# Block 0 goes last in phase one, and its last two pairs' operands reach the resident tiles by copies on the chip

## The chip, the cores and the metric

The kernel runs on one core of a Trainium2 chip. Its time is the device time of one execution in microseconds (us); a kernel's figure is the median over its runs. Engines are named as in the profile: PE (TensorE matmuls), PEld (its weight loads), DVE (VectorE), ACT (ScalarE), POOL (GpSimd) and SP (SyncE, which here only starts transfers). A "q" behind a name, as SPq, is the engine's instruction queue.

## The reference, cut to what is computed

```python
def mixer_layer(x, pool_past, pos0, norm_g, w_in, ...):
    h = rmsnorm(x, norm_g)                                  # (T, 1024)
    u, v, z_a, xb, z_b = jnp.split(h @ w_in, ...)           # w_in is (1024, 5 * 1024)
    v_n = layernorm(v, ln_v_g, ln_v_b)
    a = u * chunk_mlp(v_n, w_spatial, b_spatial) * silu(z_a)  # 8 heads, 128x128 mixing of positions
    x_ext = concatenate([pool_past, xb])
    b = pool_mix(x_ext, pos0, w_pool, pool_scale) * silu(z_b) # trailing means over 2/4/8/16 rows
    return x + concatenate([a, b]) @ w_out, x_ext[-15:], v_n
...
y = rmsnorm(mixer_layer(x, ...)[0], final_g)
```

There is one layer, with 4096 prompt tokens and 32 sample tokens, all in float32.

## The kernel before, in words

Every large product is a two-by-two block product with seven multiplications instead of eight (`NQ = 7`, numbered q). Each float32 operand is split into a rounded part and a remainder (`lo_part`), and three matmuls per 128 rows of depth form one product. One multiplication q is therefore 4 x 3 = 12 matmuls, of 128 x 512 in most places; `Combine.after(q)` takes the sums out of PSUM with copies on ACT and additions on DVE.

**Phase one.** The weights of v lie in seven resident tiles, the `slots` (`wv[q]`, one for each q). The 4096 tokens are four blocks of 1024, and a block is four `Pair`s (b, j), j = 0 to 3, of 2 x 128 tokens. `Pair.operands()` transposes a pair's normed tokens on PE and makes seven operand tiles of 4 KB a partition from them (`split`, pool `op_p`, nine buffers). Each is stored to DRAM, to `xops` for blocks 0 to 2 and to `xops_l` for block 3, and is used for v (`Pair.product`). Rows of v are normed (`norms`) and stored to `v_all` from ACT's queue (`Pair.store`, tiles `vt` of pool `v_p`, four buffers). Pairs follow each other in the order of blocks 0, 1, 2, 3. The last two, `pa` and `pb`, are taken in the order of `lagged`: (a,0) (a,1) (b,0) (a,2) (b,1) (a,3) (b,2) (a,4) (a,5) (b,3) (a,6) (b,4) (b,5) (b,6). Then come their norms and stores.

**Phase two.** For each block, 1024 columns of tokens lie as operands in the same seven slots, loaded from `xops` (`Tokens.load`, two transfers of 1 MB for each slot). Sets of weights ("pool" and "gate") pass by them. A set's weights are loaded as `raw` tiles, and `prepare` turns them into operand tiles `wop`, up to `LEAD` = 5 multiplications ahead. Results go to `t` tiles (pool `t_p`). The first group is a pair of pool sets, `groups[0]`, in lagged order; behind its (b,3) stand the spatial constants (`WT`, `bias`). All pools of phase two are opened on memory that phase one has left, and a new tile waits for the old tiles that it covers.

**Phase three.** Out products: `OutPair`s of 2 x 128 rows times `w_out`, in two halves z of the depth. `OutPair.finish` norms both row tiles and stores them to the output. For the last pair `finish(True)` runs behind the last multiplication.

Engines run their queues in order; the order within a queue is fixed when the program is built, by a planner that may move an instruction ahead of others that are not ready by its own costs.

Of the kernel before, what the change touches and what calls it, by code (L numbers as in the profile page):

```python
# [35 lines left out]
def stream_step(ctx: ExitStack, tc, x_prompt, x_sample, state_pool, norm_g, w_in, ln_v_g, ln_v_b,  # L36
# [141 lines left out]
    def stacked(acc, rows, n, terms):  # L178
# [6 lines left out]
        mm(acc[:, :n], st, wh, start=False, stop=True)  # L185


    with ExitStack() as ph:
        xt_p = ph.enter_context(tc.tile_pool(name="xt_p", bufs=4))
        g_p = ph.enter_context(tc.tile_pool(name="g_p", bufs=1))  # L190
        h_p = ph.enter_context(tc.tile_pool(name="h_p", bufs=6))
        op_p = ph.enter_context(tc.tile_pool(name="op_p", bufs=9))
        v_p = ph.enter_context(tc.tile_pool(name="v_p", bufs=4))
        ps_acc = ph.enter_context(tc.tile_pool(name="ps_acc", bufs=5, space=bass.MemoryType.PSUM))
# [19 lines left out]

        g_bc = g_p.tile([P, D], F32, name="g_bc")


# [34 lines left out]
        def load_v_weights(c):  # L252
            v_raws[c] = a, b = [op(F32).rearrange("p (k e) -> p k e", e=P) for _ in range(2)]
            c0 = D + c * P
            nc.sync.dma_start(a, w_in_v[:, :, c0:c0 + P])
            nc.sync.dma_start(b, w_in_v[:, :, c0 + 512:c0 + 512 + P])
# [169 lines left out]
        class Pair:  # L426
            def __init__(self, b, j):
                self.b, self.j = b, j

# [15 lines left out]
            def split(self, q, src):  # L445
                t = op().rearrange("p (h x) -> p h x", h=2)
                self.ops[q] = t
                nc.scalar.copy(t[:, 0, :], src)
                lo_part(t[:, 1, :], src, t[:, 0, :])
                if self.b < NB - 1:  # L450
                    dst = xops[self.b, self.j].rearrange("p (q x) -> p q x", q=NQ)[:, q, :]
                    nc.sync.dma_start(dst, t.rearrange("p h x -> p (h x)").bitcast(F32))
                else:
                    dst = xops_l[q, :, :, self.j * P:(self.j + 1) * P]
                    nc.sync.dma_start(dst, t.rearrange("p h (k t) -> p (h k) t", t=P).bitcast(F32))
# [45 lines left out]

            def store(self):
                for z, v in enumerate(self.v):
                    dst = v_all[self.b, :, :, 4 * z + self.j, :].rearrange("h p c -> p h c")
                    nc.scalar.dma_start(dst, v.rearrange("p (h c) -> p h c", c=P))

        pairs += [Pair(b, j) for b in range(NB) for j in range(4)]
        before = {0: [past.load, edge_load, lambda: load_rows(2)], 1: [lambda: load_v_weights(0), lambda: load_rows(3)],
# [18 lines left out]
        for n, pair in enumerate(pairs[:-2]):  # L527
            steps = pairs[n + 1].operands()
            pair.start()
            for q in range(NQ):  # L530
# [7 lines left out]
                pair.product(q)  # L538
        pa, pb = pairs[-2:]
        steps = pb.operands()  # L540
        pa.start()
        pb.start()
        for n, (pair, q) in enumerate(lagged(pa, pb)):
# [5 lines left out]
            pair.product(q)  # L549
        for pair in (pa, pb):  # L550
            norms([], [(v, P) for v in pair.v])
            pair.store()


    def pool(name, bufs, stack=ctx, **kw):
        return stack.enter_context(tc.tile_pool(name=name, bufs=bufs, reuse_waits="tile", **kw))

    raw_p = pool("raw_p", 6)
    op_p = pool("wop_p", 6)
    sum_p = pool("sum_p", 3)  # L560
    ps_acc2 = pool("ps_acc2", 6, space=bass.MemoryType.PSUM)

# [36 lines left out]
    class OutPair:  # L599
# [50 lines left out]
        def multiply(self, q):  # L650
            own = {0: 0, 1: 1, 2: 0, 3: 3, 4: 0, 5: 5, 6: 3}[q]
            if own == q:
                self.acc[own] = acc2_tile()
            x, w = self.ops[q], w_slots[self.z, q]
# [14 lines left out]

        def finish(self, last=False):  # L670
            t0 = 2 * self.i * P
            if self.z == 0:
                for n in range(2):
                    nc.gpsimd.dma_start(part[t0 + n * P:t0 + (n + 1) * P, :], self.y[n])  # L674
                return
            a = small("ssa", 2)
            nc.vector.tensor_tensor(a, self.ss[:, :, 0], self.ss[:, :, 1], ALU.add)
            nc.vector.tensor_scalar(a, a, 1.0 / D, EPS, ALU.mult, ALU.add)
            r = rsqrt(a, 2)
            for n in range(2):  # L680
                y = self.y[n]
                for c in (slice(0, 512), slice(512, D)) if last else (slice(0, D),):
                    nc.vector.scalar_tensor_tensor(y[:, c], y[:, c], r[:, n:n + 1], f_bc[:, c], ALU.mult, ALU.mult)
                    (nc.sync if last and n == 0 else nc.gpsimd).dma_start(yp[t0 + n * P:t0 + (n + 1) * P, c], y[:, c])  # L684

# [50 lines left out]

    def acc2_tile():
        return ps_acc2.tile([P, 512], F32, tag="acc", name="acc")

    with ExitStack() as ph:  # L740
        t_p = pool("t_p", 10, ph)
        cn_p = pool("cn_p", 1, ph)
        ps_sp = pool("ps_sp", 1, ph, space=bass.MemoryType.PSUM)
        ps_acc = ps_acc2

        def acc_tile():
            return ps_acc.tile([P, 512], F32, tag="acc", name="acc")
# [7 lines left out]
        WT = cn_p.tile([P, HEADS, 2 * P], F32R, name="WT")  # L755
        bias = cn_p.tile([P, HEADS, P], F32, name="bias")
        bias_s = cn_p.tile([P, HEADS, DEC], F32, name="bias_s")

# [16 lines left out]
        def spatial_constants(ws, bsp):  # L775
# [6 lines left out]
            for z0 in (0, P):  # L782
                nc.gpsimd.memset(WT[64:P, :, z0:z0 + 64].bitcast(F32), 0.0)
            for q in range(2):
# [47 lines left out]
        class Set:  # L832
# [4 lines left out]

            def load(self):
                i = self.i
# [9 lines left out]
                for view in views:  # L849
                    raws.append(raw_tile().rearrange("p (k e) -> p k e", e=P))  # L850
                    nc.sync.dma_start(raws[-1], view)
                self.load_v()
# [181 lines left out]

        prepare(1)
        for q in range(NQ):
            tokens[0].load(q)
        prepare(LEAD)
        constants_loaded = spatial_loads()
        at, later = 0, []  # L1040
# [31 lines left out]
    with ExitStack() as ph:  # L1072
# [47 lines left out]
        for n in range(n_sets, len(groups)):  # L1120
# [6 lines left out]
            for m, (s, q) in enumerate(order):  # L1127
                at += 1
                prepare(at + LEAD)
                if m == 0 and n in samples:  # L1130
                    samples[n].load()
                k = n - n_sets - 4
                if 0 <= k < KT and m in (0, 2):
                    state_load(k) if m == 0 else state_split()
                s.multiply(q)
                if m == 2 and ended:
                    for x in ended:
                        x.finish()
# [7 lines left out]
            if g[0].z == 0 and len(g) == 2:  # L1146
                kept, ended = [x.y for x in g], None
        for x in ended:
            x.finish(True)

# [28 lines left out]
```

## Time and profile before

| | us |
|---|---|
| median of 3 runs (lowest, highest) | 2444.87 (2441.67, 2445.24) |
| the profiled execution, own time | 2445.14 |
| its span, first to last instruction | 2443.4 |
| granted TensorE clock, mean | 0.991 |
| PE busy | 2382.9 (98% of the span), 11981 matmuls |
| DVE busy | 1865.1 (76%) |
| ACT busy | 964.7 (39%) |

The profile covers one execution. The granted clock is the share of full speed (2.4 GHz) that TensorE had; 0.50 is its lower level, 1.2 GHz. In the profile's rows "x44" counts instructions, an arrow in brackets names what ended an engine's idle time, and Lnnn is a line of the kernel before. Phase one ends at 424.5 us of the span, phase two at about 1776 us.

### The profile page before, as it was taken

The numbers are of one execution on the slowest core, as the hardware profiler recorded it, in microseconds if no ns is written. First come the engines' busy times: TensorE is split into PE (matmuls) and PEld (weight loads), VectorE is DVE, ScalarE is ACT, GpSimd is POOL, SyncE is SP. The second block draws the span as 40 slices with busy tenths as digits, with TensorE's granted clock in tenths as the row PEclk, the third lists the DMA queues.
The fourth block names the chain that finished last, engine by engine and source line by source line (L and its number), as shares of the span: only waits on it lengthen the run. The fifth ranks groups of instructions, "written<-read, shape, count | busy, mean of one in ns | idle before, by whom it ended". The sixth has DMA issues, their size and how long they took to land. (4 is left out here: it accounts for less than half of the span.)

```text
span 2443.4 us, 32978 instructions
## 1 busy us (share of the span) xinstructions
PE 2382.9 (98%) x11981; PEld 1995.0 (82%) x11981; DVE 1865.1 (76%) x3386; ACT 964.7 (39%) x1702; POOL 309.2 (13%) x462
## 2 busy tenths in 40 slices
PE   6999999899999999999999999999999999999997
PEld 5788887688878888788888799999987777888876
DVE  6887776687786877877778868678776777588886
ACT  5554453344433444433444334444322333233332
POOL 3200000011111111111112112222210000000000
PEclk8999999999999999999999999999999999999999
DMA  8677799733348323556234382335596776855542
GB/s 253 240 271 272 277 271 278 269 108 100 121 130 311 102 92 98 172 187 209 96 104 148 107 321 90 96 98 181 192 330 231 259 250 228 310 169 167 152 135 74
DMA packets 337082, 458.15 MB, mean 188 GB/s; under 512 B 19516, under 2 KB 256828, under 8 KB 334232
## 3 DMA queue, kind: packets, MB, share of 16 engines
q1 hardware_dynamic: 282296, 369.34, 45.0%
q0 software_dynamic: 20144, 65.62, 7.6%
q10 hardware_dynamic: 34480, 21.11, 3.0%
q8 instruction: 94, 1.54, 0.3%
q14 instruction: 68, 0.56, 0.1%
HBM read 280.04 MB, written 175.96 MB: 187 GB/s over the span
## 5 line engine op out<-in xcount | busy, mean ns | idle before, releaser
L174 PE MATMUL acc<-slot,wop 128*128 128x512 f32 (+1 forms) x2240 | 788.1, 352 | 11.3 <-ACT t L150 6.0
L176 PE MATMUL acc<-slot,wop 128*128 128x512 f32 (+1 forms) x2240 | 786.2, 351 | 1.4 <-DVE wop L82 1.4
L175 PE MATMUL acc<-slot,wop 128*128 128x512 f32 (+1 forms) x2240 | 785.6, 351 | 0.3 <-DMA slot<-xops 0.3
L174 PEld LDWEIGHTS acc<-slot,wop 128*128 128x128 f32 x2240 | 422.6, 189 | 74.1 <-ACT t L150 7.5
L82 DVE TENSOR_TENSOR wop<-raw,wop 128x512 fp32r<-128x512 f32 x510 | 359.1, 706 | 151.8 <-ACT wop L107 108.7
L176 PEld LDWEIGHTS acc<-slot,wop 128*128 128x128 f32 x2240 | 422.3, 189 | 61.8 <-DVE wop L82 1.9
L175 PEld LDWEIGHTS acc<-slot,wop 128*128 128x128 f32 x2240 | 422.7, 189 | 57.5 <-DMA slot<-xops 0.6
L657 PE MATMUL acc<-slot,wop 128*128 128x512 f32 x896 | 354.0, 395 | 3.8 <-DVE y L663 2.8
L658 PE MATMUL acc<-slot,wop 128*128 128x512 f32 x896 | 353.7, 395 | 0.0
L659 PE MATMUL acc<-slot,wop 128*128 128x512 f32 x896 | 353.6, 395 | 0.0
L107 ACT CAST wop<-raw 128x512 fp32r<-128x512 f32 x340 | 209.8, 621 | 281.5 <-PE acc L176 221.6
L663 DVE TENSOR_TENSOR y<-acc,y 128x512 f32<-128x512 f32 x256 | 173.7, 687 | 96.2 <-PE acc L659 95.1
L148 DVE TENSOR_TENSOR t<-acc,t 128x512 f32<-128x512 f32 (+1 forms) x320 | 184.3, 582 | 77.3 <-ACT t L157 56.3
L657 PEld LDWEIGHTS acc<-slot,wop 128*128 128x128 f32 x896 | 168.4, 188 | 46.6 <-issue 4.0
L659 PEld LDWEIGHTS acc<-slot,wop 128*128 128x128 f32 x896 | 168.4, 188 | 40.3
L658 PEld LDWEIGHTS acc<-slot,wop 128*128 128x128 f32 x896 | 168.4, 188 | 39.8
L619 ACT CAST wop<-raw 128x512 fp32r<-128x512 f32 x160 | 99.2, 621 | 240.6 <-PE acc L659 202.1
L174 PE MATMUL acc<-slot,op 128*128 128x512 f32 x448 | 181.5, 406 | 0.0
L176 PE MATMUL acc<-slot,op 128*128 128x512 f32 x448 | 177.2, 396 | 0.0
L175 PE MATMUL acc<-slot,op 128*128 128x512 f32 x448 | 176.7, 394 | 0.0
L107 ACT CAST wop<-sum 128x512 fp32r<-128x512 f32 x144 | 89.2, 620 | 212.5 <-PE acc L176 174.9
L82 DVE TENSOR_TENSOR wop<-sum,wop 128x512 fp32r<-128x512 f32 x208 | 142.7, 686 | 38.4 <-ACT wop L107 30.1
(218 smaller groups left out, 2885.5 us busy)
## 6 DMA issues: line engine op xcount, KB each, us to landing
raw<-in_w_in_dram SPq DMA_DIRECT2D x104, 512.0 KB, 4.4
xops<-op SPq DMA_DIRECT2D x84, 512.0 KB, 6.2
slot<-xops SPq DMA_DIRECT2D x42, 1024.0 KB, 11.2
abT<-t POOLq DMA_DIRECT2D x128, 256.0 KB, 2.6
raw<-abT SPq DMA_DIRECT2D x64, 512.0 KB, 4.3
wops<-wop SPq DMA_DIRECT2D x56, 512.0 KB, 3.9
slot<-wops SPq DMA_DIRECT2D x14, 2048.0 KB, 9.2
xt<-in_x_prompt_dram SPq DMA_DIRECT2D x32, 512.0 KB, 4.6
```

The lines of the kernel that those rows point to most:

```text
L82: nc.vector.tensor_tensor(out, src, hi.bitcast(F32), ALU.subtract)
L107: nc.scalar.copy(hi, src)
L148: add = lambda o, x, y: nc.vector.tensor_tensor(o, x, y, ALU.add)
L174: mm(acc, sh, mh, start=fresh and k == 0, stop=False, skip_group_check=True)
L175: mm(acc, sh, ml, start=False, stop=False, skip_group_check=True)
L176: mm(acc, sl, mh, start=False, stop=k == 3, skip_group_check=True)
L619: nc.scalar.copy(t[:, 0], src)
L657: mm(a, x[:, 0, k, :], w[:, k, 0], start=fresh and k == 0, stop=False, skip_group_check=True)
L658: mm(a, x[:, 0, k, :], w[:, k, 1], start=False, stop=False, skip_group_check=True)
L659: mm(a, x[:, 1, k, :], w[:, k, 0], start=False, stop=k == 3, skip_group_check=True)
L663: nc.vector.tensor_tensor(y, self.acc[bank], y, ALU.add)
```

## The change

Six edits. The pairs of phase one go through blocks 1, 2, 3, 0. The pairs (0,2) and (0,3), now the last two, no longer store their operands. Instead, as each slot comes free of `wv[q]`, `load_first(q)` loads the operands of (0,0) and (0,1) into it with two transfers of 512 KB and copies those of `pa` on DVE and those of `pb` on ACT; phase two starts with these slots. The four raw weight tiles of `groups[0]` are loaded from POOL's queue, and their preparation precedes the last norms and stores of v, which POOL issues too. The v tiles lie at the other end of memory and are given back only then, and `t_p`, `WT` and the biases are opened after that; one raw tile of the v weights takes a `vt` buffer instead of an `op` buffer. In phase three the last pair is ended in two parts: its first row tile behind the multiplication q = 5, its second behind q = 6, with halves of 512 columns stored from SP's and ACT's queues.

```diff
@@ pools of phase one
+    v_stack = ctx.enter_context(ExitStack())
+    v_p = pool("v_p", 4, v_stack, side="right")
...
-        v_p = ph.enter_context(tc.tile_pool(name="v_p", bufs=4))
...
-            v_raws[c] = a, b = [op(F32).rearrange("p (k e) -> p k e", e=P) for _ in range(2)]
+            v_raws[c] = a, b = [t.rearrange("p (k e) -> p k e", e=P)
+                                for t in (op(F32), op(F32) if c < 3 else vtile())]
@@ class Pair
-                self.b, self.j = b, j
+                self.b, self.j, self.direct = b, j, b == 0 and j >= 2
...
                 lo_part(t[:, 1, :], src, t[:, 0, :])
+                if self.direct:
+                    return
...
-            def store(self):
+            def store(self, queue=nc.scalar):
...
-                    nc.scalar.dma_start(dst, v.rearrange("p (h c) -> p h c", c=P))
+                    queue.dma_start(dst, v.rearrange("p (h c) -> p h c", c=P))
...
-        pairs += [Pair(b, j) for b in range(NB) for j in range(4)]
+        pairs += [Pair(b, j) for b in (1, 2, 3, 0) for j in range(4)]
@@ the last two pairs
+        def load_first(q):
+            first_ops[q] = t = slot()
+            dst = t[:, :8 * HALF].rearrange("p (h j x) -> p h j x", h=2, j=4)
+            src = xops[0].rearrange("j p (q h x) -> q h p j x", q=NQ, h=2)
+            for h in range(2):
+                nc.sync.dma_start(dst[:, h, :2].bitcast(F32), src[q, h, :, :2])
+            nc.vector.tensor_copy(dst[:, :, pa.j], pa.ops[q])
+            nc.scalar.copy(dst[:, :, pb.j], pb.ops[q])
...
             pair.product(q)
-        for pair in (pa, pb):
-            norms([], [(v, P) for v in pair.v])
-            pair.store()
+            if pair is pb:
+                load_first(q)
@@ OutPair.finish
-        def finish(self, last=False):
+        def finish(self, last=None):
...
+            tiles = (0, 1) if last is None else (last,)
...
-            for n in range(2):
+            for n in tiles:
                 y = self.y[n]
-                for c in (slice(0, 512), slice(512, D)) if last else (slice(0, D),):
-                    nc.vector.scalar_tensor_tensor(y[:, c], y[:, c], r[:, n:n + 1], f_bc[:, c], ALU.mult, ALU.mult)
-                    (nc.sync if last and n == 0 else nc.gpsimd).dma_start(yp[t0 + n * P:t0 + (n + 1) * P, c], y[:, c])
+                for z, c in enumerate((slice(0, 512), slice(512, D)) if last is not None else (slice(0, D),)):
...
+                    queue = nc.gpsimd if last is None else (nc.sync, nc.scalar)[z]
+                    queue.dma_start(yp[t0 + n * P:t0 + (n + 1) * P, c], y[:, c])
@@ phase two
-                nc.gpsimd.memset(WT[64:P, :, z0:z0 + 64].bitcast(F32), 0.0)
+                tc.keep_in_program_order(nc.gpsimd.memset(WT[64:P, :, z0:z0 + 64].bitcast(F32), 0.0))
...
-        prepare(1)
-        for q in range(NQ):
-            tokens[0].load(q)
+        tokens[0].ops = first_ops
+        for s in groups[0]:
+            loads.pop(0)[2].load(nc.gpsimd)
         prepare(LEAD)
+        for pair in (pa, pb):
+            norms([], [(v, P) for v in pair.v])
+            pair.store(nc.gpsimd)
+        v_stack.close()
+        t_p = pool("t_p", 10, ph)
...
@@ phase three
                 s.multiply(q)
+                if n == len(groups) - 1 and q == 5:
+                    s.finish(0)
...
-        for x in ended:
-            x.finish(True)
+        ended[0].finish(1)
```

## Rows read from the trace of the kernel before

**Rows 1.** Busy time of each engine over the whole span: time, share, instructions.

```profile
PE 2382.9 (98%) x11981; PEld 1995.0 (82%) x11981; DVE 1865.1 (76%) x3386; ACT 964.7 (39%) x1702; POOL 309.2 (13%) x462
```

**Rows 2.** Stretches: length, busy us (instructions) by engine, clock, DMA share, GB/s.

```profile
404.00:414.00 10.00, 10.00 (x44) 8.07 (x43) 3.68 (x6) 1.54 (x3) 0.00 (x0) 1.00 1.18 292
...
424.50:437.00 12.50, 10.32 (x36) 7.38 (x35) 12.02 (x32) 4.46 (x8) 0.00 (x0) 0.86 1.07 391
437.00:460.00 23.00, 17.02 (x66) 13.11 (x65) 4.75 (x7) 7.58 (x12) 1.53 (x7) 0.93 1.07 391
460.00:477.00 17.00, 15.63 (x69) 11.76 (x68) 16.10 (x43) 4.64 (x7) 1.57 (x7) 1.00 0.59 172
...
500.00:520.00 20.00, 19.81 (x96) 16.16 (x96) 17.97 (x27) 11.03 (x19) 3.70 (x4) 1.00 0.34 106
```

**Rows 3.** PE in order of time: start, length, instruction, idle time before it.

```profile
428.87 0.79 PE L176 MATMUL acc<-slot,wop 128*128 128x512 f32 x1 [1.44 <-DVE wop L82]
...
452.30 0.78 PE L174 MATMUL acc<-slot,wop 128*128 128x512 f32 x1 [4.78 <-ACT t L150]
```

**Rows 4.** Waits between 384 and 520 us: total, times, longest.

```profile
ACT t L150 <- DMA v_all<-vt: 7.2, 1, 7.2
```

**Rows 5.** Landing time of the v_all stores, all 32.

```profile
DMA to landing us min/median/max: 3.3/5.7/17.4
```

**Rows 6.** SP's queue in order of time.

```profile
394.17 0.38 SPq L825 DMA_DIRECT2D slot<-xops  x1
394.64 10.99 SPq L455 DMA_DIRECT2D xops_l<-op  x5
...
413.05 32.57 SPq L825 DMA_DIRECT2D slot<-xops  x13
```

**Rows 7.** Landing time of the slot loads from xops, all 42.

```profile
DMA to landing us min/median/max: 5.6/11.2/17.5
```

**Rows 8.** Transfers by line: queue, count, size of one, median us to landing.

```profile
raw<-in_w_in_dram SPq DMA_DIRECT2D x104, 512.0 KB, 4.4
...
xops_l<-xt POOLq DMA_DIRECT2D x7, 64.0 KB, 6.6
...
comb<-vt ACTq DMA_DIRECT2D x8, 512.0 KB, 2.9
...
out_dram<-y SPq DMA_DIRECT2D x2, 256.0 KB, 2.1
out_dram<-y POOLq DMA_DIRECT2D x2, 256.0 KB, 2.4
```

**Rows 9.** DVE by line and shape.

```profile
L405 DVE TENSOR_SCALAR h<-op 128x512 fp32r<-128x512 f32 x1 | 0.4, 427 | 1.1 <-PE acc L244 1.1
```

**Rows 10.** ACT by line.

```profile
L866 ACT CAST raw<-raw 128x1024 fp32r<-128x1024 f32 x32 | 33.7, 1053 | 6.0 <-DVE wop L82 5.4
```

**Rows 11.** DVE by line, 384 to 500 us.

```profile
L82 DVE TENSOR_TENSOR op<-tr,op 128x512 fp32r<-128x512 f32 x3 | 2.1, 686 | 0.9 <-ACT op L448 0.9
```

**Rows 12.** DVE in order of time, last group.

```profile
2413.34 0.16 DVE L90 TENSOR_TENSOR rs_t<-rs_y 128x2 f32<-128x2 f32 x1
2413.45 0.69 DVE L663 TENSOR_TENSOR y<-acc,y 128x512 f32<-128x512 f32 x1
...
2429.93 0.69 DVE L663 TENSOR_TENSOR y<-acc,y 128x512 f32<-128x512 f32 x1 [2.10 <-PE acc L659]
...
2434.04 2.74 DVE L683 SCALAR_TENSOR_TENSOR y<-y,rs_y,spare 128x512 f32<-128x512 f32 x4
```

**Rows 13.** POOL in order of time, last stores.

```profile
2436.41 1.21 POOL L684 DMA_DIRECT2D out_dram<-y  x2 [16.88 <-DVE y L683]
```

**Rows 14.** ACT in order of time, while the last v weights are made.

```profile
60.17 0.62 ACT L107 CAST slot<-op 128x512 fp32r<-128x512 f32 x1 [1.66 <-DMA op<-in_w_in_dram]
```

**Rows 15.** POOL in order of time, at the start.

```profile
32.68 1.26 POOL L103 TENSOR_TENSOR op<-op 128x512 f32<-128x512 f32 x1
```

**Rows 16.** DVE in order of time, at the start.

```profile
32.77 1.19 DVE L87 TENSOR_SCALAR rs_t<-na 128x2 int32<-128x2 int32 x1
```

More of the change, by code (lines that the diff above doesn't have):

```diff
@@ L185, in stacked, with pool @@
         mm(acc[:, :n], st, wh, start=False, stop=True)
+    def pool(name, bufs, stack=ctx, **kw):
+        return stack.enter_context(tc.tile_pool(name=name, bufs=bufs, reuse_waits="tile", **kw))
+    v_stack = ctx.enter_context(ExitStack())
+    v_p = pool("v_p", 4, v_stack, side="right")
     with ExitStack() as ph:
@@ L215, in stream_step @@
         g_bc = g_p.tile([P, D], F32, name="g_bc")
+        first_ops = {}
         rows_t, wraw = {}, []
@@ L549, in stream_step @@
             pair.product(q)
-        for pair in (pa, pb):
-            norms([], [(v, P) for v in pair.v])
-            pair.store()
-    def pool(name, bufs, stack=ctx, **kw):
-        return stack.enter_context(tc.tile_pool(name=name, bufs=bufs, reuse_waits="tile", **kw))
+            if pair is pb:
+                load_first(q)
     raw_p = pool("raw_p", 6)
@@ L560, in stream_step @@
     sum_p = pool("sum_p", 3)
-    ps_acc2 = pool("ps_acc2", 6, space=bass.MemoryType.PSUM)
+    ps_acc = pool("ps_acc2", 6, space=bass.MemoryType.PSUM)
     def raw_tile(dt=F32):
@@ L652, in multiply @@
             if own == q:
-                self.acc[own] = acc2_tile()
+                self.acc[own] = acc_tile()
             x, w = self.ops[q], w_slots[self.z, q]
@@ L675, in finish @@
                 return
+            tiles = (0, 1) if last is None else (last,)
             a = small("ssa", 2)
-            nc.vector.tensor_tensor(a, self.ss[:, :, 0], self.ss[:, :, 1], ALU.add)
+            ss, a = self.ss[:, tiles[0]:tiles[-1] + 1], a[:, :len(tiles)]
+            nc.vector.tensor_tensor(a, ss[:, :, 0], ss[:, :, 1], ALU.add)
             nc.vector.tensor_scalar(a, a, 1.0 / D, EPS, ALU.mult, ALU.add)
-            r = rsqrt(a, 2)
-            for n in range(2):
+            r = rsqrt(a, len(tiles))
+            for n in tiles:
                 y = self.y[n]
-                for c in (slice(0, 512), slice(512, D)) if last else (slice(0, D),):
-                    nc.vector.scalar_tensor_tensor(y[:, c], y[:, c], r[:, n:n + 1], f_bc[:, c], ALU.mult, ALU.mult)
-                    (nc.sync if last and n == 0 else nc.gpsimd).dma_start(yp[t0 + n * P:t0 + (n + 1) * P, c], y[:, c])
+                for z, c in enumerate((slice(0, 512), slice(512, D)) if last is not None else (slice(0, D),)):
+                    nc.vector.scalar_tensor_tensor(y[:, c], y[:, c], r[:, n - tiles[0]:n - tiles[0] + 1], f_bc[:, c],
+                                                   ALU.mult, ALU.mult)
+                    queue = nc.gpsimd if last is None else (nc.sync, nc.scalar)[z]
+                    queue.dma_start(yp[t0 + n * P:t0 + (n + 1) * P, c], y[:, c])
     class OutSample:
@@ L735, in multiply @@
             nc.gpsimd.dma_start(ys, self.y)
-    def acc2_tile():
-        return ps_acc2.tile([P, 512], F32, tag="acc", name="acc")
     with ExitStack() as ph:
[L741 to L747, printed above, removed]
         def temp(dt=F32):
@@ L753, in few @@
             return t_p.tile([P, HALO + DEC], F32, tag="few", name="few", bufs=3)
-        WT = cn_p.tile([P, HEADS, 2 * P], F32R, name="WT")
-        bias = cn_p.tile([P, HEADS, P], F32, name="bias")
-        bias_s = cn_p.tile([P, HEADS, DEC], F32, name="bias_s")
         def spatial_loads():
@@ L836, in __init__, with load @@
                 self.tok, self.kind, self.i, self.ops, self.stage = tok, kind, i, {}, tok.b
-            def load(self):
+            def load(self, queue=nc.sync):
                 i = self.i
@@ L850, in load @@
                     raws.append(raw_tile().rearrange("p (k e) -> p k e", e=P))
-                    nc.sync.dma_start(raws[-1], view)
+                    queue.dma_start(raws[-1], view)
                 self.load_v()
@@ L1033, in prepare @@
                 done += 1
-        prepare(1)
-        for q in range(NQ):
-            tokens[0].load(q)
+        tokens[0].ops = first_ops
+        for s in groups[0]:
+            loads.pop(0)[2].load(nc.gpsimd)
         prepare(LEAD)
+        for pair in (pa, pb):
[3 more added lines that the diff above has]
+        t_p = pool("t_p", 10, ph)
+        cn_p = pool("cn_p", 1, ph)
+        ps_sp = pool("ps_sp", 1, ph, space=bass.MemoryType.PSUM)
+        WT = cn_p.tile([P, HEADS, 2 * P], F32R, name="WT")
+        bias = cn_p.tile([P, HEADS, P], F32, name="bias")
+        bias_s = cn_p.tile([P, HEADS, DEC], F32, name="bias_s")
         constants_loaded = spatial_loads()
```

## The prediction

> **What bounds the kernel now.** The page's first part comes first: PE is busy 98% of the span [rows 1], so an edit can win only where PE stands still or runs at its lower clock. The table of stretches around the end of phase one, at 424.5 us, shows such a place. In an undisturbed stretch PE starts 44 matmuls in 10 us, one per 0.227 us. From 424.5 to 437 us it starts 36, worth 8.2 us, in 12.5: 4.3 lost. From 437 to 460 it starts 66, worth 15.0, in 23: 8.0 lost. From 460 to 477 it starts 69, worth 15.7, in 17: 1.3 lost [rows 2]. Idle time is one part of this; the granted clock's mean of 0.86 and 0.93 is the other: after each of the two long gaps PE ran at 1.2 GHz for a while. In the first stretch that cost (1 - 0.86) x 12.5 = 1.7 us [rows 2].
>
> PE in order of time gives the two gaps: 1.44 us until DVE has a remainder of a weight operand, 4.78 us until ACT's copy into a t tile has emptied a bank [rows 3]. The waits say what ACT stood for: 7.2 us for a store of v to DRAM [rows 4], since the t tile lies on an old v tile. The longest of these stores took 17.4 us where the median is 5.7 [rows 5]: from 424.5 to 460 us the DMA share is 1.07, at 391 GB/s [rows 2], that is, the DMA engines are full. SP's queue says with what, and why the weights were late: stores of the last pair's operands, each waiting for its operand, hold the queue from 394.64 until 405.6; only then come the four raw weight loads, and from 413.05 to 445.6 thirteen slot loads of 1 MB [rows 6].
>
> At the other end the last addition starts at 2429.93; its chain of small operations reaches the output multiplications at 2434.04, and POOL issues the last two stores from 2436.41 on [rows 12, 13].
>
> **The end of phase one, first stretch.** The two direct pairs drop 14 stores of 512 KB, and the slots take 7 MB from DRAM instead of 14. The stores that held SP are gone; the raw loads stand in POOL's queue, which is empty there. Their tiles lie on x tiles whose last transposes are over by about 391.4 us (one multiplication of 12 x 0.227 = 2.7 us ahead of 394.17, when the first slot comes free [rows 6]). They land 4.4 us after issue if they cost what they do on SP, 6.6 if they cost what POOL's transfers in 1024 pieces took [rows 8]; by 405 either way, some 20 us ahead of use. What can stay of the 4.3 us: the weight operands lie partly on op tiles that now live until their copy, the last copies end near 426, and five operands must be made while the copies run. I leave 0.8 us of the 4.3 (bounds 0 and 4.3): win 3.5.
>
> **Second stretch.** The new t tiles lie on op tiles, free once copied, not on v tiles, and with 14 MB of traffic less the stores of v no longer queue behind 13 MB of slot loads. The 8.0 us go, but DVE must follow: from 424.5 to 477 it was busy 12.02 + 4.75 + 16.10 = 32.9 us; if PE does the same in 52.5 - 12.3 = 40.2 us, DVE is at 82%. From 500 to 520 it was at 90%, and PE lost only 0.2 [rows 2]. So I leave 1.0 (bounds 0 and 8.0): win 7.0. The 1.3 us from 460 to 477 belong to the spatial constants, with DVE busy 16.1 of 17 [rows 2]; I leave them whole (bounds 0 and 1.3).
>
> **The added copies.** Seven copies of 1024 elements on DVE: the one SBUF-to-SBUF operation with one tensor input took 0.43 us for 512 [rows 9], so between that and 0.85; I take 0.7, 4.9 us in all. Seven on ACT at 1.05 [rows 10], 7.4 us. Over the 30 us of the last pair there is room: from 404 to 414 DVE was busy 3.68 of 10 and ACT 1.54 [rows 2]. If that room were not there, all 12.3 us could land on PE.
>
> One copy is on a tight path. Seven operands of pa and two of pb fill the nine op buffers, so operand 1 of pb must wait until `load_first(0)` has copied operand 0, and that waits for the slot, free at 394.17 [rows 6]. (b,1) is due one multiplication later, 2.7 us. ACT's copy 1.05, a cast of 512 (half of it, 0.53) and the remainder 0.69 [rows 10, 11] make 2.3, before hand-overs and whatever stands ahead in two queues. I take 0.3 us lost (bounds 0 and 1.5, one more cast and remainder ahead). Behind (b,1) PE alone waits; the later operands have two products or more.
>
> POOL also issues the four stores of v and then clears WT, which must wait for these stores. Behind that stand POOL's halo copies of the first pool sets; the first of these sets ends eleven multiplications, 30 us, after 424.5, so I cost this at nothing; were the stores as late as 17.4 us [rows 5] it would still be covered.
>
> A rule of the skill speaks against this arrangement. The start of the kernel shows the effect in one form: with POOL at a two-input operation of 1.26 us [rows 15], DVE's operations of a few elements take 1.19 us [rows 16] instead of 0.16 [rows 12]. The Trainium skill (SBUF — State Buffer, section SBUF: two separate sides) says that the two share a port pair as a lock, and that a float32 copy within SBUF on DVE keeps POOL from writing the descriptors of its own transfers. By that rule each of four raw loads could be held for one DVE copy, 0.7 us, so they would land 2.8 us later, and the sum stands. That it would show as late weights is a rival below, and no row here shows a POOL transfer held in this way.
>
> **The start.** One raw tile of the last v weights now waits for a v tile. ACT stood 1.66 us for that load [rows 14]. Gone, it wins 1.7 at most; if the v tile comes free one store of comb later, it costs 2.9 [rows 8]. I take 0.
>
> **The end.** Only two of four output multiplications (2.74 us, [rows 12]) stay behind the last chain: 1.4 us less. The last store is issued by ACT as its half is ready, not as POOL's second (half of 1.21 us later, [rows 13]), and lands in 2.1 instead of 2.4 us [rows 8]. Before: 2436.41 + 0.6 + 2.4 = 2439.4. After: 2434.04 + 1.4 + 2.1 = 2437.5, a win of 1.9. But the first row tile's chain runs from one product earlier: add to multiplication is 4.1 us, so its two multiplications fall on 2431.3 to 2432.7, in the middle of the second's chain, and can hold it by up to 1.4. DVE's queue does place other work inside such a chain [rows 12]. Were the last addition placed behind all of it, it would start 2.8 us late: 0.9 slower. Between 1.9 and -0.9 I take 1.2.
>
> **The sum.** 3.5 + 7.0 - 0.3 + 0 + 1.2 = 11.4 us. The profiled execution took 2445.14, so 2433.7; its excess over the median, 0.27, does not matter here, and from the median, 2444.87, it is 2433.5. With every bound at its good end: 12.3 + 1.3 + 1.9 + 1.7 = 17.2, or 2427.7.
>
> **Rivals.** (1) The copies into a slot wait for the transfers into the same slot. For it: the transfers are issued first and the regions interleave. Against it: the bytes do not overlap. Then (b,1) waits for a landing, about 5 us (between the 4.4 of a 512 KB load and the fastest slot load, 5.6 [rows 7, 8]), and 1.7 for the clock: 2440.2. (2) The change does not do what it says: t tiles or WT still wait for stores of v, which now come later in the queue. For it: the 17.4 [rows 5]; against it: the DMA engines have lost the traffic that made it. The 7.0 stay: 2440.5. (3) The weights come late by POOL's queue. Trace: POOL's pieces took 6.6 us for 64 KB [rows 8]; against it, 20 us of slack. The 3.5 stay: 2437.0. (4) Slower: rival 1 with a landing as under full queues. Slot loads took 11.2 us in the median and 17.5 at most [rows 7]. With 17.5 it is 2433.5 + 17.5 + 1.7 = 2452.7; all is lost from a landing of 9.7 us on, and it is measurably slower from 14.6. Against it: the last pair no longer stores, and DMA has half the load.
>
> **Chances and range.** The forecast 0.70, rival 1 0.11, rival 2 0.08, rival 3 0.05, rival 4 0.06. A measurement tells 0.2%, 4.9 us, from no change: faster is below 2440.0. Forecast and rival 3 lie there, and rivals 1 and 2, which sit on the bound, with about a quarter of their 0.19: 0.80. The same is the rest of them, 0.14; slower 0.06. The forecast's own range is 2428 to 2438; held 8 times in 10 the range goes from 2428, the sum of good ends, to 2441, where rivals 1 and 2 lie.
>
> **What would show it.** Right: around the end of phase one no PE gap over 1 us, the clock at 1.00, DMA share well under 1; raw loads on POOL near 392 us; no ACT wait for a store of v; last output store issued by ACT near 2 us sooner after the last addition. Wrong: a gap before (b,1) (rival 1, 4), PE waiting for an ACT copy into t (2), for a weight operand (3), or DVE full and PE idle at the constants; a start of the products later than before; or the gain eaten by small waits elsewhere, which this trace cannot show.

## Result and the profile after

The changed kernel takes 2430.45 us (median of 6 runs, 2428.78 to 2435.85) beside 2445.01 for the kernel before on the same chip (6 runs, 2441.67 to 2446.74): a ratio of 0.9946, 95% interval 0.9933 to 0.9958. The forecast was 2433.5, with a range of 2428 to 2441. The time is inside; two of the terms behind it were the wrong size, and one was right although the runs refute one of its two reasons.

The same stretches as in [rows 2], of the profiled execution after (span 2429.1 us):

```profile
404.00:414.00 10.00, 10.00 (x44) 8.04 (x44) 4.56 (x8) 2.77 (x5) 2.64 (x3) 1.00 0.82 241
...
424.50:437.00 12.50, 10.44 (x39) 7.71 (x38) 11.98 (x29) 6.33 (x10) 1.85 (x2) 0.86 0.66 242
437.00:460.00 23.00, 21.75 (x98) 17.35 (x97) 11.75 (x23) 11.91 (x18) 4.20 (x12) 1.00 0.49 138
460.00:477.00 17.00, 16.08 (x68) 12.12 (x67) 16.83 (x52) 3.43 (x6) 0.76 (x2) 1.00 0.23 70
```

Counted as in the prediction, at 0.227 us for a matmul: the first stretch loses 12.5 - 39 x 0.227 = 3.6 us (4.3 before), the second 23 - 98 x 0.227 = 0.8 (8.0 before), the third 17 - 68 x 0.227 = 1.6 (1.3 before). The DMA share of 1.07 is gone; the clock of the second stretch is back at 1.00, that of the first is not. PE in order of time, against [rows 3], with the idle time in brackets:

```profile
427.04 0.50 PE L174 MATMUL acc<-slot,wop 128*128 128x512 f32 x1 [2.06 <-ACT wop L107]
...
428.75 0.63 PE L174 MATMUL acc<-slot,wop 128*128 128x512 f32 x1
```

The gap of 4.78 us is gone. The first gap has grown from 1.44 to 2.06 us, and it now waits for ACT's cast of the first weight operand; the matmuls behind it start 0.43 us apart where 0.23 is normal, so the clock falls here as before. ACT's queue, in order of time, shows what the cast stood behind:

```profile
423.16 2.37 ACT L298 ACTIVATE vt<-vt,nb,rs_y 128x1024 f32<-128x1024 f32 x2
425.44 1.03 ACT L557 CAST slot<-op 128x1024 fp32r<-128x1024 f32 x1
426.38 1.66 ACT L107 CAST wop<-raw 128x512 fp32r<-128x512 f32 x3
```

Two normalisations of v, then the seventh copy into a slot, then the first three casts. The seventh slot holds the v weights of phase one's last product, whose last matmul starts at 424.58, so the copy could not come much sooner; the normalisations, which end at 425.5, could have come later. SP's queue, against [rows 6], holds no store any more, and POOL's has the raw loads and the stores of v:

```profile
394.20 12.07 SPq L555 DMA_DIRECT2D slot<-xops  x6
...
419.40 6.48 SPq L555 DMA_DIRECT2D slot<-xops  x6
```

```profile
373.17 0.93 POOL L855 DMA_DIRECT2D raw<-comb  x1 [273.54 <-PE tr L448]
408.48 0.89 POOL L855 DMA_DIRECT2D raw<-in_w_in_dram  x1 [34.38 <-DVE op L82]
...
442.32 0.89 POOL L513 DMA_DIRECT2D v_all<-vt  x1 [15.54 <-ACT vt L298]
```

Three of the four raw loads were held until 408.5, not issued near 392 as forecast: the second one's tile lies on a half tile that DVE was still reading. Against [rows 12], the end on DVE, and the queues of the last four stores on ACT and SP:

```profile
2418.90 0.69 DVE L678 TENSOR_TENSOR y<-acc,y 128x512 f32<-128x512 f32 x1
...
2420.47 1.41 DVE L700 SCALAR_TENSOR_TENSOR y<-y,rs_y,spare 128x512 f32<-128x512 f32 x2
...
2424.30 1.41 DVE L700 SCALAR_TENSOR_TENSOR y<-y,rs_y,spare 128x512 f32<-128x512 f32 x2
2421.91 4.19 ACTq L703 DMA_DIRECT2D out_dram<-y  x2
2421.24 4.17 SPq L703 DMA_DIRECT2D out_dram<-y  x2
```

From the last addition to the end of the last multiplication it is 2424.30 + 1.41 - 2418.90 = 6.81 us; before it was 2434.04 + 2.74 - 2429.93 = 6.85. The first tile's two multiplications fell into the middle of the second's chain, and what the split took off the end it put back there. From the last multiplication to the end of the span, though, it is 3.4 us where it was 6.6. Stretches that part at the last byte, in the columns of [rows 2], show what most of this is (before, then after):

```profile
2434.80:2439.20 4.40, 0.00 (x0) 0.00 (x0) 1.98 (x3) 0.00 (x0) 1.09 (x2) 0.50 0.63 238
2439.20:2443.40 4.20, 0.00 (x0) 0.00 (x0) 0.00 (x0) 0.00 (x0) 0.00 (x0) 0.50 0.00 0
```

```profile
2421.20:2427.40 6.20, 0.00 (x0) 0.00 (x0) 4.06 (x17) 0.00 (x0) 0.00 (x0) 0.52 0.45 169
2427.40:2429.10 1.70, 0.00 (x0) 0.00 (x0) 0.00 (x0) 0.00 (x0) 0.00 (x0) 0.50 0.00 0
```

The bytes are out 2439.2 - 2436.8 = 2.4 us after the last multiplication before the change and 2427.4 - 2425.7 = 1.7 after it, 0.7 sooner. The other 2.5 us lie behind the last byte, in a stretch in which no engine and no transfer shows any work: 4.2 us before, 1.7 after.

To place gains in all runs, each span is cut at starts of PE's products, read from the groups of PE by line. For the kernel after these are the last start of phase one (424.1) and the first spatial product (483.2):

```profile
L174 PE MATMUL acc<-slot,op x448: 388/395/496, 84.8 to 424.1; 128*128 128x512 f32 x150
L912 PE MATMUL sp<-WT,raw x256: 277/279/392, 483.2 to 1640.8; 128*128 128x256 f32 x128
```

The two others are the first and last start of the output products. Four pieces result, in us: the passage (last product of phase one to first spatial product), the middle, phase three, and the end.

| kernel | passage | middle | phase three | end | median, us | ratio to before, interval |
|---|---|---|---|---|---|---|
| before | 66.0 | 1286.6 | 652.8 | 13.9 | 2445.01 | |
| after | 59.1 | 1286.7 | 648.4 | 10.8 | 2430.45 | 0.9946, 0.9933 to 0.9958 |
| tail_only | 65.7 | 1285.4 | 651.6 | 10.4 | 2438.30 | 0.9982, 0.9974 to 0.9991 |
| queue_only | 66.0 | 1285.8 | 652.2 | 10.4 | 2440.99 | 0.9988, 0.9978 to 0.9998 |
| no_tail | 59.1 | 1286.1 | 650.9 | 11.8 | 2432.29 | 0.9960, 0.9948 to 0.9973 |
| copy_pool | 61.4 | 1286.0 | 650.3 | 10.7 | 2433.63 | 0.9967, 0.9955 to 0.9978 |
| v_old | 57.6 | 1284.3 | 649.3 | 10.8 | 2427.16 | 0.9942, 0.9929 to 0.9954 |
| v_only | 65.6 | 1286.1 | 651.1 | 13.9 | 2443.44 | 1.0005, 0.9996 to 1.0014 |
| no_copy | 66.6 | 1286.8 | 651.5 | 10.4 | 2439.22 | 0.9992, 0.9983 to 1.0000 |
| raws_sp | 59.2 | 1284.1 | 651.5 | 10.6 | 2430.13 | 0.9950, 0.9937 to 0.9964 |
| shift_only | 65.0 | 1288.1 | 651.6 | 13.9 | 2442.06 | 0.9998, 0.9990 to 1.0006 |
| no_shift | 59.0 | 1285.3 | 651.0 | 10.8 | 2430.42 | 0.9953, 0.9939 to 0.9967 |
| better | 59.2 | 1283.9 | 651.3 | 10.6 | 2430.05 | 0.9952, 0.9939 to 0.9966 |
| norms_later | 57.1 | 1287.3 | 654.1 | 10.7 | 2431.99 | 0.9951, 0.9938 to 0.9965 |

The pieces are of one execution each; the medians and ratios are of 5 to 12 runs beside runs of the kernel before (whose median in the other calls was 2443.66, 2442.05, 2441.98 and 2442.59). The passage and the end repeat within about 1 us among kernels that are alike there: those two pieces, 6.9 and 3.1 us, are the change's. The middle and phase three move by 4 and 6 us without any system. In the first pair of profiles phase three gave 4.4 us, which reads like an effect of the change; over all runs it is 651.1 to 652.8 in the five kernels with the old front and 648.4 to 654.1 in the nine others.

### The profile page after: what moved, and what is told of

The parts are those of the page before. It is cut to its first block, busy times and chain, and to the rows that moved or that the text cites. A ratio compares the mean times of both kernels' runs of the same rounds, so it can differ in the third digit from the quotient of the medians.

```text
span 2429.1 us, 32966 instructions
## 1 busy us (share of the span) xinstructions
PE 2379.2 (98%) x11981; PEld 1994.0 (82%) x11981; DVE 1872.6 (77%) x3406; ACT 971.6 (40%) x1709; POOL 309.9 (13%) x468
## 5 line engine op out<-in xcount | busy, mean ns | idle before, releaser
L175 PEld LDWEIGHTS acc<-slot,wop 128*128 128x128 f32 x2240 | 422.2, 188 | 57.1
## 6 DMA issues: line engine op xcount, KB each, us to landing
slot<-xops SPq DMA_DIRECT2D x28, 1024.0 KB, 10.4
```

The costliest lines, as they stand in the source:

```text
L175: mm(acc, sh, ml, start=False, stop=False, skip_group_check=True)
```

## Experiments

**The end: split or queue.** tail_only puts the change's end on the kernel before; queue_only moves only the last four stores to other queues, with no split:

```
-  (nc.sync if last and n == 0 else nc.gpsimd).dma_start(...)
+  ((nc.sync, nc.scalar)[c.start // 512] if last else nc.gpsimd).dma_start(...)
```

> The kernel before with the last pair of phase three ended in two parts and its stores on SP's and ACT's queues; nothing else. Theory A (the prediction's): the two output multiplications that leave the last chain are the win, up to 1.4 us, the queue little: 1.2 us faster than before, 1.9 at most. Theory B (the trace after): the chain on DVE is as long as before, 6.8 us from the last addition to the last multiplication's end, and the win is the queue, since after POOL's last store the span went on for 5.8 us and after ACT's for 3.0: 3.1 us faster. The waits of PE in phase three stay as before.

> The kernel before with the last four stores on SP's and ACT's queues instead of SP's and POOL's; the last pair is still ended in one piece. Theory A: at most 0.9 us faster than before (0.6 for the issue, 0.3 for the landing). Theory B: 2.5 to 3.1 us faster, as much as with the two parts.

Both end 10.4 us after the last output product's start, against 13.9. So the queue gives the whole gain of this piece and the split none; the medians lie 2.7 us apart, but their intervals overlap. In queue_only the last store is issued at 2432.58 + 1.68 and the span ends at 2437.0, 2.7 us later; before, POOL's last issue was over at 2437.62 [rows 13] and the span ended 5.8 us later. Behind the last byte queue_only has 1.4 us and tail_only 1.3, so of the 3.5 us by which the piece shrinks some 2.8 lie there.

```profile
2431.14 2.74 DVE L683 SCALAR_TENSOR_TENSOR y<-y,rs_y,spare 128x512 f32<-128x512 f32 x4
2432.58 1.68 ACTq L684 DMA_DIRECT2D out_dram<-y  x2
```

no_tail is the kernel after with the old end.

> The changed kernel with the old end. Theory A: 1.2 us slower than the changed kernel. Theory B: 3.1 us slower, so about 11.4 us faster than before, 7.3 of it at the end of phase one and 4.4 in phase three.

The passage stays at 59.1: the front's gain stands alone. The time is 1.8 us above the change's, but the intervals overlap. Its end is 11.8, not 13.9, though its code is that of before; POOL's last issue ends at 2427.11 and the span at 2430.8, 3.7 us later. The last byte is out 2.3 us after the last multiplication, as late as before; the difference lies behind it:

```profile
2428.60:2430.80 2.20, 0.00 (x0) 0.00 (x0) 0.00 (x0) 0.00 (x0) 0.00 (x0) 0.50 0.00 0
```

The old end leaves 4.2 to 4.3 us there in all three kernels that have it with the old front (before, v_only, shift_only) and 2.2 with the new one; the stores on SP and ACT leave 1.3 to 1.8 with either. So the queue is worth 1 to 3.5 us: 0.7 are bytes that are out sooner, and the rest is a stretch whose cause stays open.

**The first gap: ACT's seventh copy on POOL.** copy_pool makes that one copy with `nc.gpsimd.tensor_copy`.

> The changed kernel with the seventh copy of pb on POOL instead of ACT. In the changed kernel PE stood 2.06 us at the start of phase two for the first cast of a weight operand, which stood in ACT's queue behind this copy, and then ran at the lower clock. Theory C (the queue's order): the cast starts 0.9 us or more earlier, PE's gap shrinks to about 1.2 us, and if the clock then stays up 1.7 us more are won: 0.9 to 2.6 us faster than the changed kernel. Theory D (the weights land late, or their tiles come free late): no change, within 0.3 us.

Neither theory came true. The passage got longer, not shorter, 61.4 (the median is 3.2 us above the change's, with intervals that barely overlap); the clock of the first stretch is 0.73, and PE waits 1.11 and 0.51 us for casts and 1.45 for a remainder. Read from the programs' allocation, the second and third weight operands (bytes 182624 to 186720 and 178528 to 182624 of a partition) lie partly on the operand that the seventh copy reads (180576 to 184672), so they wait for this copy on whatever engine it is:

```profile
425.32 1.14 ACT L107 CAST wop<-raw 128x512 fp32r<-128x512 f32 x2 [0.63 <-POOL slot L558]
```

DVE and POOL in order of time show a second price:

```profile
424.28 1.57 DVE L556 CAST slot<-op 128x1024 fp32r<-128x1024 f32 x1
```

```profile
424.24 1.05 POOL L558 CAST slot<-op 128x1024 fp32r<-128x1024 f32 x1
```

DVE's copy, 0.69 us elsewhere, took 1.57 beside POOL's: POOL's ends at 425.29, 1.01 us after DVE's began. This agrees with the rule of the Trainium skill (SBUF — State Buffer, section SBUF: two separate sides) by which whichever of the two starts first has the shared ports for its whole instruction.

**The second gap: place or traffic.** The prediction gave two reasons for the 7.0 us: t tiles off the v tiles, and half the bytes. Five kernels tell them apart. v_old is the kernel after with the v tiles back in the phase's stack and their last stores ahead of the weights; v_only is the kernel before with the v tiles alone moved and their last stores put behind the first weights (the edit of v_only; that of v_old is the reverse):

```
+    v_stack = ctx.enter_context(ExitStack())
+    v_p = pool("v_p", 4, v_stack, side="right")
...
-        v_p = ph.enter_context(tc.tile_pool(name="v_p", bufs=4))
```

> The kernel after, with the v tiles back in their old place between the operand tiles and the second phase's memory, and the last stores of v ahead of the first weights. The stretch from phase one's last product to the first spatial product took 66.0 us in the kernel before and 59.1 in the kernel after. If the place of the v tiles was what PE waited for (the forecast's second stretch), ACT's copy into a t tile waits for a store of v again and the stretch is 63 to 66 us. If it was only the 14 MB of traffic that held those stores, the stores land in 3 to 4 us, no gap over 2 us comes back and the stretch is 59 to 60.

> The kernel before, with the v tiles alone moved to the far end and their last stores put behind the first weights; all operands still go through DRAM in the old order of blocks. If the place of the v tiles was what PE waited for, the 4.78 us gap before the t tile goes and the stretch from phase one's last product to the first spatial product falls from 66.0 to about 60; the first gap of 1.44 us stays. If the full DMA engines were the cause, the stretch stays at 64 to 66, because something else that is stored or loaded is then waited for.

The move wins nothing either way. v_old keeps the whole gain and 1.5 us more (57.6: the change's wait of 1.25 us for ACT at 447.03 is not there), and v_only has none of it (65.6): in v_only PE's long wait of before is back, with one for a slot ahead of it.

```profile
439.92 0.50 PE L175 MATMUL acc<-slot,wop 128*128 128x512 f32 x1 [2.01 <-DMA slot<-xops]
...
452.28 0.80 PE L174 MATMUL acc<-slot,wop 128*128 128x512 f32 x1 [5.30 <-ACT t L150]
```

no_copy is the kernel after with the on-chip copies alone undone (`self.direct = False`, whole loads in `load_first`).

> The kernel after, with its new order of blocks, its v tiles at the far end and its weight loads on POOL, but no on-chip copies: the last two pairs are stored to DRAM and the slots loaded whole from there, as before. The difference to the kernel after is what the copies are worth. If placement did the work, the stretch from phase one's last product to the first spatial product is 59 to 60.5 us; if the halved traffic did, it is 63 to 66 us with the DMA share back near 1 from 424 to 460 us. A third possibility is a start of phase two that waits for a slot load, since the last slots can be loaded only when the last operand is in DRAM: a PE gap of 3 us or more at the first products of phase two.

The gain of the passage is gone (66.6), though ACT no longer waits for a store of v. PE waits for the slots instead. SP's queue and the stretches say why: the last eight slot loads go out from 416.6 to 439.4, behind the stores, and the DMA engines are full again. The copies also spare the last operands the way through DRAM, for which SP stands 5.2 us here; but from 410 to 449 us the DMA share is never under 1.01 in any 3 us, so it is the bytes that set the pace. No run halves them without the copies.

```profile
443.20 0.77 PE L174 MATMUL acc<-slot,wop 128*128 128x512 f32 x1 [4.13 <-DMA slot<-xops]
448.24 0.80 PE L175 MATMUL acc<-slot,wop 128*128 128x512 f32 x1 [4.26 <-DMA slot<-xops]
```

```profile
416.60 22.82 SPq L555 DMA_DIRECT2D slot<-xops  x8
```

```profile
424.50:437.00 12.50, 11.98 (x51) 9.49 (x51) 12.38 (x32) 4.42 (x8) 0.11 (x1) 1.00 1.04 394
437.00:460.00 23.00, 14.60 (x54) 11.00 (x53) 4.04 (x7) 6.05 (x9) 4.20 (x12) 0.78 0.99 342
```

One thing was still open: v_only also leaves the second t tile under a v tile. By the allocation the far end is only 3.7 KB further on, and that t tile (bytes 212448 to 214624) still overlaps a v tile; which pair's v this is hangs on an edit that looks like a detail, the raw tile taken from the ring of v tiles, which moves the ring on by one. With it, as in the kernel after and in v_old, the t tile covers only v tiles of the pair before the last, which are stored some 17 us sooner. shift_only puts this edit alone into the kernel before, no_shift takes it alone out of the kernel after:

```
-            v_raws[c] = a, b = [op(F32).rearrange(...) for _ in range(2)]
+            v_raws[c] = a, b = [t.rearrange(...) for t in (op(F32), op(F32) if c < 3 else vtile())]
```

> The kernel before with one edit: the second raw tile of the fourth v weights is taken from the ring of v tiles. The place of the ring stays; which tile of the ring the last two pairs get moves on by one. Read from the programs' allocation, the second t tile (bytes 212448 to 214624 of a partition) then overlaps the two v tiles of the pair before the last, whose stores are issued near 423 us, and none of the last pair, whose stores are issued near 440. Theory ring (the wait was for whichever pair's v lay under that t tile): ACT's wait of 7.2 us for a store of v goes, and the stretch from phase one's last product to the first spatial product falls from 66.0 us to between 58 and 62. Theory traffic (the full DMA engines): the wait moves to slot loads and the stretch stays between 64 and 67, the time between 2440 and 2444.

> The kernel after with one edit undone: the second raw tile of the fourth v weights comes from the operand tiles again, so that the ring of v tiles stands where it stood before. The v tiles are still at the far end and half the traffic is gone, but the second t tile now overlaps a v tile of the last pair, whose stores POOL issues at about 442.3 us. Theory ring: ACT's copy into that t tile waits until such a store has landed, near 449, PE stands 2 to 6 us before 450 and the stretch from phase one's last product to the first spatial product is 62 to 66 us in place of 59.1. Theory traffic: it stays at 59 to 60.

In shift_only ACT's wait for a store of v does go, and the second stretch loses only 23 - 92 x 0.227 = 2.1 us. The passage still takes 65.0: PE now stands 2.04 and 2.90 us for the spatial constants, whose loads SP issues only behind the thirteen slot loads, and the third stretch loses 17 - 45 x 0.227 = 6.8.

```profile
437.00:460.00 23.00, 21.76 (x92) 16.79 (x90) 6.92 (x12) 10.44 (x16) 0.57 (x2) 1.00 1.07 392
460.00:477.00 17.00, 11.55 (x45) 8.84 (x46) 14.73 (x41) 1.77 (x3) 2.51 (x11) 0.90 0.66 192
```

```profile
414.27 33.09 SPq L826 DMA_DIRECT2D slot<-xops  x13
447.41 3.25 SPq L767 DMA_DIRECT2D raw<-in_w_spatial_dram  x1
```

In no_shift the t tile does lie on the last pair's v, and POOL waits for its store before the halo copy:

```profile
440.70 0.89 POOL L512 DMA_DIRECT2D v_all<-vt  x1 [15.42 <-ACT vt L297]
...
444.70 0.20 POOL L976 COPY t<-carry 128x16 f32<-128x16 f32 x1 [1.79 <-DMA v_all<-vt]
```

The store has landed within 4 us, the t tile is needed at 444.75, and the passage is 59.0. The place under the t tile shows as a wait of about 5 us with full DMA engines and costs nothing with half the traffic. Of the three theories only traffic is left: place and ring fall. tail_only, whose program is that of before up to phase three, fits this: there the clock stayed at 1.00 and the first stretch lost 12.5 - 43 x 0.227 = 2.7 us and not 4.3, and the passage was 65.7 all the same.

```profile
424.50:437.00 12.50, 10.59 (x43) 8.00 (x44) 12.41 (x33) 5.21 (x10) 0.00 (x0) 1.00 1.07 392
```

**The raw loads.** raws_sp issues the first four raw weight loads from SP (`loads.pop(0)[2].load()`).

> The kernel after, with the first four raw weight loads on SP's queue in place of POOL's. If POOL's queue was harmless (the forecast), the time is that of the kernel after within 1 us. If the loads on POOL came late (in the trace of the kernel after three of them stood 34 us behind a tile that was still read), SP's queue lets them in earlier or just as late, and the first stretch loses less than 3.6 us: up to 2 us faster. If SP's queue puts them behind the last slot loads, which wait for the last operands, the weights come 5 us or more later and the first stretch loses 2 to 5 us more.

The passage is 59.2 and the gap 2.06 again: POOL's queue cost nothing. The loads are no sooner from SP (issued between 405.3 and 412.5 us), where the second one waits for the same half tile.

**Taking the first gap away.** better puts the sums' memory below that of the weight operands, leaves the seventh operand's copies to SP's DMA queue and queues the normalisations behind the third weight operand:

```
-    op_p = pool("wop_p", 6)
     sum_p = pool("sum_p", 3)
+    op_p = pool("wop_p", 6)
...
+            if q == NQ - 1:
+                nc.sync.dma_start(dst[:, :, pb.j].bitcast(F32), pb.ops[q].bitcast(F32))
+                nc.sync.dma_start(dst[:, :, pa.j].bitcast(F32), pa.ops[q].bitcast(F32))
...
+            with tc.issue_after(hi.ins):
                 norms([], [(v, P) for v in pair.v])
```

> The kernel after with the first products of phase two freed from the last copies: the memory of the sums put below that of the weight operands, so that the first three operands lie on tiles that are free early; the seventh operand's two copies made by SP's DMA queue in place of DVE and ACT; the norms of the last two pairs queued behind the first three weight operands on ACT (the last pair's on DVE too). If ACT's queue and the overlaid tiles are what makes PE stand 2.06 us at 427 and then run at a mean clock of 0.86, the gap falls below 0.5 us, the clock is 1.00, and the stretch from phase one's last product to the first spatial product falls from 59.1 to 55.5 to 57 us. If DVE, busy 11.98 of 12.5 us there, is the bound, the loss comes back as waits for remainders of weight operands and the stretch stays at 58 to 60.

The gap falls to 0.97 us and the first stretch to a loss of 12.5 - 50 x 0.227 = 1.2, at a clock of 1.00. The second loses it again, 23 - 86 x 0.227 = 3.5:

```profile
424.50:437.00 12.50, 11.55 (x50) 9.39 (x51) 6.96 (x14) 3.93 (x5) 1.78 (x2) 1.00 0.67 226
437.00:460.00 23.00, 19.43 (x86) 15.01 (x85) 15.76 (x38) 12.81 (x20) 5.11 (x12) 1.00 0.59 169
```

The waits name the new stall, the fourth weight operand, which lies on the seventh operand's tile and now waits for a DMA copy (DVE then stands 5.5 us for ACT's cast, so DVE's work is not the bound there):

```profile
ACT wop L109 <- DMA slot<-op: 8.3, 1, 8.3
```

The passage is 59.2, unchanged: a cheaper start, paid for some 15 us later. norms_later, on v_old's placing, keeps the copies on DVE and ACT and only puts off the normalisations (with the same swap of memory). Its base is thus v_old, not the change.

> The kernel after with the v tiles in their old place (the run that gave 57.6 us for the stretch from phase one's last product to the first spatial product), the sums' memory below that of the weight operands, and the norms of the last two pairs queued behind the third weight operand on ACT and, for the last pair, behind the second remainder on DVE; all seven copies stay on DVE and ACT. Only the seventh copy, 1.05 us, and one cast of 0.6 now stand between the last product and the first one of phase two. If ACT's queue is what PE waits for, the gap falls from 2.06 us to 1.0 to 1.6, and if that is short enough the clock stays at 1.00: the stretch is 54.5 to 56.5. If DVE's work is the bound, what is put off comes back later, as in the run before: 57 to 58.5.

The gap is 1.65 us, 0.41 less: the seventh copy starts 0.43 us behind phase one's last matmul where it was 0.86. That is the share of the normalisations; the rest is the copy and the cast. The clock of the stretch is 1.00 with 47 matmuls in it. But the passage is 57.1, only 0.5 less than v_old's, in the range of the second expectation (57 to 58.5). The second stretch loses 23 - 98 x 0.227 = 0.8 us where v_old, with 105 matmuls, loses none.

```profile
424.50:437.00 12.50, 10.85 (x47) 8.38 (x46) 12.09 (x33) 7.33 (x11) 1.78 (x2) 1.00 0.81 269
437.00:460.00 23.00, 21.75 (x98) 17.41 (x97) 13.21 (x28) 12.06 (x19) 4.20 (x12) 1.00 0.48 138
```

Nor can the clock be booked to the shorter gap. tail_only, whose program there is that of before, kept 1.00 after a gap of 1.50 us where the kernel before fell to half speed after 1.44:

```profile
428.16 0.50 PE L176 MATMUL acc<-slot,wop 128*128 128x512 f32 x1 [1.50 <-DVE wop L82]
```

The time shows no gain: 2431.99, five runs from 2426.91 to 2436.68. So v_old, 2427.16, is the fastest kernel measured, but its interval overlaps that of the change; that it beats the change is not shown.

## Why the prediction was right, step by step

- **First stretch, 3.5 us of 4.3.** This step failed: 0.7 came. The prediction took the overlay of weight operands and last copies for 0.8 us; it missed that ACT's in-order queue puts two normalisations and the seventh copy, which cannot begin before phase one's last product has read its slot, ahead of the first cast. The gap moved from DVE's remainder to ACT's cast and grew, and the drop of the clock, (1 - 0.86) x 12.5 = 1.7 us, stayed. better and norms_later, which free that cast in two ways (gaps of 0.97 and 1.65 us), show what sets the gap. But their passages are 0.1 us longer and 0.5 shorter than those of their own bases, the change and v_old; that a shorter gap there is worth time is not shown.
- **Second stretch, 7.0 of 8.0.** 7.2 came. Of the two reasons given, the first, new t tiles off the v tiles, does not hold for the kernel as built: by the allocation the second t tile still lies on a v tile, of the pair before the last. Traffic alone did it: no_shift keeps the gain with the t tile under the last pair's v, v_old keeps it with the v tiles in their old place, v_only and shift_only have the new place or its effect without the gain, no_copy loses the gain with the new place. That DVE would follow was right.
- **The constants, 1.3 left.** 1.6 with the change. shift_only shows that this was no fixed amount: as long as slot loads fill SP's queue, the constants are the next to be late.
- **The lagged pair, 0.3 lost; the copies.** Nothing was lost: 44 matmuls from 404 to 414 us before and after. A copy took 0.69 us on DVE and 1.05 on ACT, as assumed.
- **The start, 0.** The first product of phase one's pairs starts at 84.8 instead of 85.1, within what the other runs scatter (83.3 to 86.3).
- **The end, 1.2.** The term was too small, and its working wrong: the split gave 0.04 us, as the bound of 1.4 lost in the middle of the second's chain said it might, and leaving POOL's queue gave 3.1 in the pair of profiles, not the 0.5 that the issue and the medians to landing [rows 8] allowed. For the bytes alone the 0.5 was near: they are out 0.7 us sooner, and the sum for the kernel before, 2439.4, ends where its last byte moves, at about 2439.1. What the sum left out is the rest of the span, 4.0 us from there to 2443.4, which it put at nothing without giving a reason; it shrank by 2.5, and why stays open.
- **The sum.** The two solid pieces give 6.9 + 3.1 = 10.0 us of the 11.4 forecast. The measured difference of the medians, 14.6 in the first comparison, has more in it: raws_sp and no_shift, within 0.4 us of the change's time, lie 11.6 to 11.9 below their runs of before. What is beyond 10 sits in phase three and the middle, where one profile cannot tell it from scatter; that stays open. The forecast came near partly by luck, because the first stretch's error (2.8 too much) and the end's (1.9 too little) nearly cancel.
- **Rivals.** 1 and 4: no copy waited for its slot's transfer, and no gap stands before the last pair's second operand. 2: neither ACT nor WT waited for a store of v. 3: the weights were not late by POOL's queue (raws_sp), and on POOL each raw load took 0.88 to 0.93 us to issue; the 2.06 us are ACT's.

## What to carry to other kernels

When full DMA engines make everything behind them late, removing the wait that shows only uncovers the next one: of the edits at the end of phase one, only the copies, which halve the bytes, moved the passage by 7 us, while freeing the tile that PE seemed to wait for gave 1. Work that is put off at a change of phases must be priced by the in-order queue that it joins, since a seventh copy of 1 us, which had to wait for phase one's last product, held the first matmul for 2. Losses counted stretch by stretch do not add up to time where a later wait takes them back: a gap 0.4 to 1.1 us shorter and a clock of 1.00 moved the passage by 0.5 us at most. A sum for the end of a kernel should be held against the end of its span: this one stopped 4 us short of it, and most of the end's gain lay there. A gain in a piece that the edit does not touch (4.4 us of phase three here) should be looked for in other kernels' profiles before it is explained.

## What the runs showed of the hardware

- With a transfer issued last from POOL the span ended 5.8 us (before, v_only, shift_only) and 3.7 us (no_tail) after the issue was over; with the last from ACT it took 2.6 to 3.0, though the median from issue to landing differed by only 0.3 [rows 8]. The difference is almost all behind the last byte: 4.2 to 4.3 us, 2.2, and 1.3 to 1.8.
- The length of a gap alone does not tell what the clock does. After 1.44 us [rows 3] and 2.06 us the matmuls ran at half speed, after 1.50 us (tail_only, the same program there as before) and 1.65 us (norms_later) the stretch stayed at 1.00:

```profile
428.27 0.50 PE L175 MATMUL acc<-slot,wop 128*128 128x512 f32 x1 [1.65 <-ACT wop L109]
```

- A store of 512 KB that took 17.4 us beside full DMA engines [rows 5] landed in 4.0 us when their share was 0.52 from 437 to 460 us (no_shift).
